# Two matmuls in place of three for the mixers' projections, the halves of the output added on ScalarE and VectorE

## The chip, the cores and the metric

The kernel runs on one core of a Trainium2 chip. The metric is the time of one execution on the device in microseconds, the median of several runs. TensorE (PE) multiplies out of SBUF into PSUM; ScalarE (ACT), VectorE (DVE) and GpSimd (POOL) work on tiles of 128 partitions; SyncE (SP) starts the DMA transfers. Each engine takes its instructions in the order of its own queue.

## The reference, cut to what matters

Two layers; each is a SwiGLU FFN, a mixing block and a second FFN, on 256 tokens of 1024 features in float32.

```
u = rms_norm(h, ln_mix[l])
z, xbc, dt_raw, cq, ckv, kr, gates = split_cols(u @ w_in[l], IN_SPLIT_SIZES)
y_ssd = ssd_branch(z, xbc, dt_raw, ...)      # conv + silu of xbc, chunked scan, gated by silu(z), norm, @ w_ssd_out
y_mla = mla_branch(cq, ckv, kr, cos, sin, ...)   # norm(cq) @ w_uq, norm(ckv) @ w_ukv, 8 heads, @ w_mla_out
g = jax.nn.sigmoid(gates.astype(jnp.float32)).astype(h.dtype)
merged = g[..., :D_MODEL] * y_ssd + g[..., D_MODEL:] * y_mla
h = h + merged @ w_o[l]
```

## The kernel before

All products with weights are made in float32r, in which an operand is split in a high part and a low part. An activation tile `X` holds for each 128 features both parts side by side, 256 columns each (`operand` writes them: ScalarE casts the high part, VectorE subtracts it for the low part). A weight block, 128 output features of 1024 input features as a rule, is loaded by one DMA into `st`; `ahead` casts it on ScalarE to `wh` (L151) and subtracts on VectorE to `wl` (L152). There are four buffers each of `st`, `wh` and `wl`, so a block is split when TensorE has finished the fourth block before it. The product is high x high + high x low + low x high, accumulated over the eight tiles of 128 input features in one of four PSUM buffers `g` (`gps`), which are used in turn.

Two helpers issue it. `mm` (L168 to L170) uses three matmuls of 256 columns for each tile of weights: `wh` with the high part, `wh` with the low part, `wl` with the high part, all into the same 256 columns. `mm2` (L177, L178) streams both parts of X behind one load of `wh`, 512 columns, and then `wl` with the high part, 256 columns into the first half; the two halves of the buffer add up to the product, and `halves` (L181, L182) adds them: a ScalarE copy of the second half to SBUF and a VectorE add of the first half. The FFNs, the gates inside the mixing block and `wso` use `mm2`; the dt and rotary key block `dk`, the first two gates, the six latents `lat`, the convolved blocks `bc` and `xs`, the blocks `z`, and `wmo` and `wo` use `mm`. So does the last output tile of all, which doesn't change.

The mixing block `mix` begins with the row factor of the tokens (`row_factor`: a sum over features on TensorE, L240, then nine small VectorE instructions, L248 and L215 to L223), while TensorE runs dk, two gates and latent 0. VectorE then splits weights, writes the scaled operand X for the loop (L454, L458), and the latents' operands into tile A (L204). `query` (L694) and `keyval` (L718) multiply these latents with the up-projections; each takes two PSUM buffers. Then comes the loop over eight steps of the scan (`ssd`, in which L632 writes xdt) and eight heads, with blocks of bc, xs, z and gates among them, then the merge (wso and wmo for eight output tiles) and wo. The instructions of each engine are put in order ahead of time by a scheduler with its own model of durations; on the chip each engine goes through its queue in that order.

Of the kernel before, what the change touches and what calls it, by code (L numbers as in the profile page):

```python
# [39 lines left out]
# columns of the per-layer vector block  # L40
# [15 lines left out]
# columns of the constant block  # L56
# [4 lines left out]
class Build:  # L61
# [17 lines left out]
    def plan(self):  # L79
        """every weight block in the order of its use"""  # L80
# [62 lines left out]
    def ahead(self, most=WBUF):  # L143
        """loads blocks and splits each in two float32r parts, ahead of their use"""
        while self.split_n < min(self.used + most, len(self.blocks)):
            k, src, n, w = self.blocks[self.split_n]
            st = self.stp.tile([P, 1024], F32, name="st", tag="st")[:, :n]
            self.nc.sync.dma_start(st, src)
            wh = self.whp.tile([P, 1024], F32R, name="wh", tag="wh")[:, :n]
            wl = self.wlp.tile([P, 1024], F32R, name="wl", tag="wl")[:, :n]  # L150
            self.nc.scalar.copy(wh, st)  # L151
            self.nc.vector.tensor_tensor(out=wl, in0=st, in1=wh.bitcast(F32), op=ALU.subtract)  # L152
            self.ready[self.split_n] = (k, wh.rearrange("p (k c) -> p k c", c=w), wl.rearrange("p (k c) -> p k c", c=w))
            self.split_n += 1
# [17 lines left out]
    def mm2(self, out, w, nk, X, x0, start, stop):  # L172
        """one load of the high weights serves both parts of X; the halves of out add up to the product"""
        wh, wl = w
        mm = self.nc.tensor.matmul
        for k in range(nk):
            mm(out, lhsT=wh[:, k, :], rhs=X[:, x0 + k, :], start=start and k == 0, stop=False)  # L177
            mm(out[:, :T], lhsT=wl[:, k, :], rhs=X[:, x0 + k, :T], start=False, stop=stop and k == nk - 1)  # L178
# [28 lines left out]
    def rsqrt(self, x, n, tag):  # L207
        """1 / sqrt(x): exponent trick, one tuned Newton step, one step of third order"""
# [26 lines left out]
    def row_ms(self, acc, scale, tag):  # L235
        """mean of squares + eps, tokens on partitions: [P, 2]"""
# [133 lines left out]
    def post_h(self, n, X, gain):  # L370
        """square and operand of feature tile n of the residual for the next block"""
        if n == 0:
            self.acc = self.tmp("acc", [P, T], bufs=1)
        self.operand(X, n, self.hT[:, n, :], gain[:, n:n + 1])
        self.square_into(self.acc, self.hT[:, n, :], n == 0)

# [42 lines left out]
    def mix(self, l, X0, Xn, gain, gain_next):  # L419
# [9 lines left out]
        def latent(i):  # L429
            q = int(i > 3)  # L430
            ps = self.gps()[:, :T]
            self.mm(ps, self.w("lat"), KD, X0, 0, True, True)
            o = V_QL + i
            self.operand(A, 16 + i, ps, v[:, o:o + 1])
            self.square_into(acc2[q], ps, i in (0, 4))

# [1 line left out]
        with self.tc.issue_after(self.last):  # L438
            ps = self.gps()[:, :T]
            self.mm(ps, self.w("dk"), KD, X0, 0, True, True)  # L440
            pg = self.gps()
            for g in range(2):
                self.mm(pg[:, g * T:(g + 1) * T], self.w("gate"), KD, X0, 0, g == 0, g == 1)
            latent(0)
        Rb = self.bcast(Rt, None)
        gg = self.tmp("g0", [P, 2, T], bufs=1)
        nc.scalar.copy(gg, pg.rearrange("p (g t) -> p g t", g=2))
        dk = self.tmp("ta", [P, T])
        nc.scalar.copy(dk, ps)
# [106 lines left out]
        for n in range(KD):  # L556
# [9 lines left out]
            ps = self.gps()[:, :T]  # L566
            self.mm(ps, self.w("wmo"), 8, oT, 0, True, True)
            tt(out=m, in0=gg[:, 1, :], in1=ps, op=ALU.mult)
            tt(out=m, in0=m, in1=gg[:, 0, :], op=ALU.add)
            self.operand(M, n, m)  # L570
        for n in range(KD):
            ps = self.gps()[:, :T]
            self.mm(ps, self.w("wo"), 8, M, 0, True, True)
            tt(out=self.hT[:, n, :], in0=self.hT[:, n, :], in1=ps, op=ALU.add)
# [11 lines left out]
    def conv_pair(self, S, key, cis, out):  # L586
        """out = 2 * silu(conv) for two feature tiles"""
        nc, v = self.nc, S["v"]
        y = self.tmp("cy", [P, 2, T])
        for i, ci in enumerate(cis):  # L590
            ps = self.gps()[:, :T]
            self.mm(ps, self.w(key), KD, S["X"], 0, True, True)
# [72 lines left out]
    def z(self, S, j):  # L665
        nc = self.nc
        ps = self.gps()
        for i in range(2):
            self.mm(ps[:, i * T:(i + 1) * T], self.w("z"), KD, S["X"], 0, i == 0, i == 1)
        ps = ps.rearrange("p (g t) -> p g t", g=2)  # L670
        z = self.tmp("zz", [P, 2, T], bufs=ZB)
        nc.scalar.activation(out=z, in_=ps, func=AF.Tanh, scale=0.5)
        nc.vector.scalar_tensor_tensor(out=z, in0=z, scalar=1.0, in1=ps, op0=ALU.add, op1=ALU.mult)
# [10 lines left out]
    def query(self, S, p):  # L684
        """queries of two heads, tokens on partitions"""
# [21 lines left out]
    def keyval(self, S, p):  # L707
        """keys and values of two heads, tokens on partitions; the row factors of queries and keys"""
# [132 lines left out]
def _pack(w, nb):  # L841
    """[L, K, N] -> [L, N/(128 nb), 128, nb * K/128 * 128]: one contiguous run per partition and chunk"""
# [66 lines left out]
```

## Time and profile before

| what | value |
|---|---|
| time, median of 3 runs | 1484.74 us (1484.6 to 1485.36) |
| profiled execution: span from first to last instruction | 1480.6 us |
| median less that span | 4.1 us |
| TensorE, VectorE, ScalarE busy | 1469.6, 1119.8, 908.6 us |
| granted TensorE clock, mean | 1.000 |

The page gives no other time for the profiled execution than its span; the median is that of executions timed without the profile. A matmul's end is modelled in the trace, and a matmul overlaps the next, so the price of one is read from the starts of a run of them, not from its duration.

### The profile page before, as it was taken

Reading aid. Unit: us, or ns where it says so; the run is one execution under the profiler, and the core shown is the slowest. Engines: PE = TensorE matmul, PEld = TensorE weight load, DVE = VectorE, ACT = ScalarE, POOL = GpSimd, SP = SyncE. Lnnn points to the kernel's source line nnn. Section 1 sums busy time; section 2 is a strip of 40 time slices with the busy share of each in tenths; the row PEclk is TensorE's granted clock in tenths of the full one; section 3 lists DMA queues with packets and bytes.
Section 4 is the critical chain, followed back from the end, with each engine's and each line's share of the span. In section 5 each row is a group of like instructions: output and inputs, shape, how many; then the busy total and the mean of one; then the engine's idle time right before and its main releaser. Section 6 shows DMA issues by size and latency. Waiting matters only on the chain.

```text
span 1480.6 us, 25069 instructions
## 1 busy us (share of the span) xinstructions
PE 1469.6 (99%) x9482; PEld 1313.5 (89%) x9482; DVE 1119.8 (76%) x2089; ACT 908.6 (61%) x1736; POOL 0.2 (0%) x4
## 2 busy tenths in 40 slices
PE   7999999999999999999999999999999999999999
PEld 6888899888888998888888888998888889988888
DVE  7877679888776667777677876898887676777764
ACT  6655566887765455555455554668787654555542
POOL 0000000000000000000000000000000000000000
PEclk9999999999999999999999999999999999999999
DMA  7555655333344555556655566553434445555563
GB/s 258 189 188 172 202 178 175 134 128 122 129 142 157 185 178 187 192 191 180 194 189 193 190 184 191 175 164 123 138 126 136 142 162 188 182 185 188 190 193 116
DMA packets 73353, 252.98 MB, mean 171 GB/s; under 512 B 8337, under 2 KB 10641, under 8 KB 73233
## 3 DMA queue, kind: packets, MB, share of 16 engines
q1 hardware_dynamic: 73232, 251.39, 52.7%
q8 instruction: 74, 1.21, 0.3%
q14 instruction: 47, 0.38, 0.1%
HBM read 250.31 MB, written 1.05 MB: 170 GB/s over the span
## 4 chain that ended last, share of the span: by engine, by line
PE 99%; DMA 0%; DVE 0%; ACT 0%; issue 0%; SPq 0%; ACTq 0%; DVEq 0%
PE g L177 40%; PE g L178 20%; PE g L168 9%; PE g L169 9%; PE g L170 9%; PE g L694 2%; PE s L657 2%; PE g L718 2%; PE h L779 1%; PE h L778 1%; PE s L640 1%; PE h L802 1%; PE h L760 0%; PE s L629 0%; PE h L798 0%; DMA hT<-in_x_dram 0%
## 5 line engine op out<-in xcount | busy, mean ns | idle before, releaser
L151 ACT CAST wh<-st 128x1024 fp32r<-128x1024 f32 (+2 forms) x488 | 502.9, 1031 | 495.2 <-PE g L177 309.1
L152 DVE TENSOR_TENSOR wl<-st,wh 128x1024 fp32r<-128x1024 f32 (+2 forms) x488 | 581.5, 1192 | 258.8 <-ACT wh L151 254.5
L177 PE MATMUL g<-X,wh 128*128 128x512 f32 x928 | 329.3, 397 | 7.9 <-DVE X L204 7.5
L177 PE MATMUL g<-A,wh 128*128 128x512 f32 x938 | 327.6, 395 | 0.0
L178 PE MATMUL g<-X,wl 128*128 128x256 f32 x928 | 263.1, 284 | 0.0
L178 PE MATMUL g<-A,wl 128*128 128x256 f32 x938 | 260.6, 278 | 0.0
L177 PE MATMUL g<-oT,wh 128*128 128x512 f32 x704 | 244.5, 392 | 0.0
L168 PE MATMUL g<-X,wh 128*128 128x256 f32 x768 | 220.5, 288 | 0.0
L169 PE MATMUL g<-X,wh 128*128 128x256 f32 x768 | 219.7, 286 | 0.0
L170 PE MATMUL g<-X,wl 128*128 128x256 f32 x768 | 218.5, 285 | 0.0
L177 PEld LDWEIGHTS g<-X,wh 128*128 128x128 f32 x928 | 175.3, 189 | 47.8 <-DVE X L204 8.2
L177 PEld LDWEIGHTS g<-A,wh 128*128 128x128 f32 x938 | 175.7, 188 | 40.1
L178 PE MATMUL g<-oT,wl 128*128 128x256 f32 x704 | 196.9, 280 | 0.0
L178 PEld LDWEIGHTS g<-X,wl 128*128 128x128 f32 x928 | 176.9, 191 | 1.2 <-issue 0.3
L178 PEld LDWEIGHTS g<-A,wl 128*128 128x128 f32 x938 | 176.6, 188 | 0.4
L177 PEld LDWEIGHTS g<-oT,wh 128*128 128x128 f32 x704 | 131.6, 187 | 28.6
L168 PEld LDWEIGHTS g<-X,wh 128*128 128x128 f32 x768 | 146.3, 191 | 2.9 <-issue 1.5
L169 PEld LDWEIGHTS g<-X,wh 128*128 128x128 f32 x768 | 146.5, 191 | 2.4 <-issue 0.7
L170 PEld LDWEIGHTS g<-X,wl 128*128 128x128 f32 x768 | 146.5, 191 | 0.7 <-issue 0.2
L178 PEld LDWEIGHTS g<-oT,wl 128*128 128x128 f32 x704 | 133.0, 189 | 0.2
L170 PE MATMUL g<-oT,wl 128*128 128x256 f32 x272 | 76.8, 285 | 0.0
L169 PE MATMUL g<-oT,wh 128*128 128x256 f32 x272 | 76.7, 283 | 0.0
(288 smaller groups left out, 1849.1 us busy)
## 6 DMA issues: line engine op xcount, KB each, us to landing
st<-in_w_dram SPq DMA_DIRECT2D x238, 512.0 KB, 4.3
st<-in_win_dram SPq DMA_DIRECT2D x124, 512.0 KB, 3.8
st<-in_wso_dram SPq DMA_DIRECT2D x32, 512.0 KB, 4.2
st<-in_w_dram SPq DMA_DIRECT2D x32, 384.0 KB, 3.2
st<-in_wmo_dram SPq DMA_DIRECT2D x16, 512.0 KB, 4.1
st<-in_wo_dram SPq DMA_DIRECT2D x16, 512.0 KB, 3.5
st<-in_wuq_dram SPq DMA_DIRECT2D x16, 384.0 KB, 3.3
st<-in_wukv_dram SPq DMA_DIRECT2D x8, 512.0 KB, 3.8
```

Source lines behind the costliest of these rows:

```text
L151: self.nc.scalar.copy(wh, st)
L152: self.nc.vector.tensor_tensor(out=wl, in0=st, in1=wh.bitcast(F32), op=ALU.subtract)
L168: mm(out, lhsT=wh[:, k, :], rhs=xh, start=start and k == 0, stop=False)
L169: mm(out, lhsT=wh[:, k, :], rhs=xl, start=False, stop=False)
L170: mm(out, lhsT=wl[:, k, :], rhs=xh, start=False, stop=stop and k == nk - 1)
L177: mm(out, lhsT=wh[:, k, :], rhs=X[:, x0 + k, :], start=start and k == 0, stop=False)
L178: mm(out[:, :T], lhsT=wl[:, k, :], rhs=X[:, x0 + k, :T], start=False, stop=stop and k == nk - 1)
L640: nc.tensor.matmul(pbs[q][:, i * T:(i + 1) * T], lhsT=self.E[64 * q:64 * q + 64, h:h + 1].to_broadcast([64, P]), rhs=S["HL"][64 * q:64 * q ...
L657: nc.tensor.matmul(py[64 * i:64 * i + 64, q * T + c * P:(q + 1) * T], lhsT=xdt[:, c, f:f + 64], rhs=r[:, i, o:o + n], start=q == 0 and c = ...
L694: nc.tensor.matmul(pc[c], lhsT=aa, rhs=ww, start=k == 0 and i == 0, stop=k == 3 and i == 2)
L718: nc.tensor.matmul(pc[c], lhsT=aa, rhs=ww[:, k, :], start=k == 0 and i == 0, stop=k == 1 and i == 2)
L778: mm(o, lhsT=qkT[:, 0, cs], rhs=qkT[:, 1, ks], start=c == 0, stop=False)
```

## The change

The nine projections that used `mm` in the mixing block use `mm2`, each with a full PSUM buffer of 512 columns. `halves` puts the sum into an SBUF tile, and what read PSUM before reads this tile: the latents' operand and square (tile `cy`, two buffers), the convolution (tile `sq`, two buffers), z (its own tile), dk, the first gates, and the product with `wmo`. For `wo` there is no tile: VectorE adds both halves to the residual `hT` in two instructions. The two copies that emptied the first gates and dk are gone. z takes two PSUM buffers where two groups shared one. Lines of comment fell out of the file too, and line numbers shift by up to 7.

```diff
         def latent(i):
             q = int(i > 3)
-            ps = self.gps()[:, :T]
-            self.mm(ps, self.w("lat"), KD, X0, 0, True, True)
+            ps = self.gps()
+            self.mm2(ps, self.w("lat"), KD, X0, 0, True, True)
+            lat = self.tmp("cy", [P, 2, T])[:, 0, :]
+            self.halves(lat, ps)
             o = V_QL + i
-            self.operand(A, 16 + i, ps, v[:, o:o + 1])
-            self.square_into(acc2[q], ps, i in (0, 4))
+            self.operand(A, 16 + i, lat, v[:, o:o + 1])
+            self.square_into(acc2[q], lat, i in (0, 4))
...
         with self.tc.issue_after(self.last):
-            ps = self.gps()[:, :T]
-            self.mm(ps, self.w("dk"), KD, X0, 0, True, True)
-            pg = self.gps()
+            ps = self.gps()
+            self.mm2(ps, self.w("dk"), KD, X0, 0, True, True)
+            dk = self.tmp("ta", [P, T])
+            self.halves(dk, ps)
+            gg = self.tmp("g0", [P, 2, T], bufs=1)
             for g in range(2):
-                self.mm(pg[:, g * T:(g + 1) * T], self.w("gate"), KD, X0, 0, g == 0, g == 1)
+                ps = self.gps()
+                self.mm2(ps, self.w("gate"), KD, X0, 0, True, True)
+                self.halves(gg[:, g, :], ps)
             latent(0)
         Rb = self.bcast(Rt, None)
-        gg = self.tmp("g0", [P, 2, T], bufs=1)
-        nc.scalar.copy(gg, pg.rearrange("p (g t) -> p g t", g=2))
-        dk = self.tmp("ta", [P, T])
-        nc.scalar.copy(dk, ps)
...
-            ps = self.gps()[:, :T]
-            self.mm(ps, self.w("wmo"), 8, oT, 0, True, True)
-            tt(out=m, in0=gg[:, 1, :], in1=ps, op=ALU.mult)
+            ps = self.gps()
+            self.mm2(ps, self.w("wmo"), 8, oT, 0, True, True)
+            self.halves(m, ps)
+            tt(out=m, in0=gg[:, 1, :], in1=m, op=ALU.mult)
...
-            ps = self.gps()[:, :T]
-            self.mm(ps, self.w("wo"), 8, M, 0, True, True)
-            tt(out=self.hT[:, n, :], in0=self.hT[:, n, :], in1=ps, op=ALU.add)
+            ps = self.gps()
+            self.mm2(ps, self.w("wo"), 8, M, 0, True, True)
+            for o in (0, T):
+                tt(out=self.hT[:, n, :], in0=self.hT[:, n, :], in1=ps[:, o:o + T], op=ALU.add)
...
         for i, ci in enumerate(cis):
-            ps = self.gps()[:, :T]
-            self.mm(ps, self.w(key), KD, S["X"], 0, True, True)
+            pg = self.gps()
+            self.mm2(pg, self.w(key), KD, S["X"], 0, True, True)
+            ps = self.tmp("sq", [P, T])
+            self.halves(ps, pg)
...
-        ps = self.gps()
+        z = self.tmp("zz", [P, 2, T], bufs=ZB)
         for i in range(2):
-            self.mm(ps[:, i * T:(i + 1) * T], self.w("z"), KD, S["X"], 0, i == 0, i == 1)
-        ps = ps.rearrange("p (g t) -> p g t", g=2)
-        z = self.tmp("zz", [P, 2, T], bufs=ZB)
-        nc.scalar.activation(out=z, in_=ps, func=AF.Tanh, scale=0.5)
-        nc.vector.scalar_tensor_tensor(out=z, in0=z, scalar=1.0, in1=ps, op0=ALU.add, op1=ALU.mult)
+            ps = self.gps()
+            self.mm2(ps, self.w("z"), KD, S["X"], 0, True, True)
+            self.halves(z[:, i, :], ps)
+        th = self.tmp("t2", [P, 2, T])
+        nc.scalar.activation(out=th, in_=z, func=AF.Tanh, scale=0.5)
+        nc.vector.scalar_tensor_tensor(out=z, in0=th, scalar=1.0, in1=z, op0=ALU.add, op1=ALU.mult)
```

The scheduler puts the new instructions into the queues. On VectorE, at the head of layer 0's mixing block, this stood around the operand of latent 3 (L204 that reads g_2292; g_2251 is latent 2, g_2341 latent 4; L152 splits weights, L458 writes X):

```order
L204 SCALAR_TENSOR_TENSOR A_2068<-g_2251,vec0_85,A_2068 128x256
L508 TENSOR_SCALAR dtd_2459<-dte_2456 128x64
L233 TENSOR_TENSOR Rb_2069<-Rb_2069,sq_2243 128x256
L152 TENSOR_TENSOR wl_2345<-st_2342,wh_2344 128x768
L204 SCALAR_TENSOR_TENSOR A_2068<-g_2292,vec0_85,A_2068 128x256
L458 TENSOR_TENSOR X_2204<-t2_2287,X_2204 128x2x256
L458 TENSOR_TENSOR X_2204<-t2_2328,X_2204 128x2x256
L509 RECIPROCAL dtd_2459<-dtd_2459 128x64
L152 TENSOR_TENSOR wl_2379<-st_2376,wh_2378 128x1024
L204 SCALAR_TENSOR_TENSOR A_2068<-g_2341,vec0_85,A_2068 128x256
L559 TENSOR_SCALAR g0_2200<-g0_2200 128x256
```

and this now, at the add and the operand of latent 3 (PSUM buffer g_2258, sum in cy_2281; cy_2245 holds latent 2):

```order
L510 TENSOR_SCALAR dtd_2410<-dte_2407 128x64
L460 TENSOR_TENSOR X_2180<-t2_2253,X_2180 128x2x256
L152 TENSOR_TENSOR wl_2335<-st_2332,wh_2334 128x1024
L460 TENSOR_TENSOR X_2180<-t2_2289,X_2180 128x2x256
L561 TENSOR_SCALAR g0_2097<-g0_2097 128x256
L152 TENSOR_TENSOR wl_2452<-st_2449,wh_2451 128x1024
L182 TENSOR_TENSOR cy_2281<-cy_2281,g_2258 128x256
L511 RECIPROCAL dtd_2410<-dtd_2410 128x64
L204 SCALAR_TENSOR_TENSOR A_2068<-cy_2245,vec0_85,A_2068 128x256
L233 TENSOR_TENSOR Rb_2069<-Rb_2069,sq_2250 128x256
L512 TENSOR_TENSOR dte_2407<-dte_2407,dtd_2410 128x64
L204 SCALAR_TENSOR_TENSOR A_2068<-cy_2281,vec0_85,A_2068 128x256
```

Both last X operands (L460) and two splits of 1024 columns now stand ahead of what first reads latent 3; the operands of latents 2 and 3 stand behind its add.

On TensorE, at the end of latent 5 (g_2331) and the start of the query block (L701, L694 before), the queue now reads as follows; g_2461 and g_2462 are the query's two PSUM buffers, in turn those of latents 2 and 3:

```order
L178 MATMUL g_2331<-oT_1558,wl_2226 128x256
L701 MATMUL g_2461<-wh_2261,A_2068 128x384
L701 MATMUL g_2461<-wl_2262,A_2068 128x384
L701 MATMUL g_2461<-wh_2261,A_2068 128x384 x2
L701 MATMUL g_2461<-wl_2262,A_2068 128x384
L701 MATMUL g_2461<-wh_2261,A_2068 128x384
L701 MATMUL g_2461<-wh_2305,A_2068 128x384
L701 MATMUL g_2461<-wl_2306,A_2068 128x384
L701 MATMUL g_2462<-wh_2261,A_2068 128x384
L701 MATMUL g_2462<-wl_2262,A_2068 128x384
```

Eight matmuls into the first buffer now stand ahead of the first into the second. Earlier in this queue, the row sum L240 stood behind 44 matmuls of the triples of dk and the first gate, and stands behind 35 matmuls of pairs now.

## Rows read from the trace of the kernel before

**Rows 1.** The page: the span, and each engine's busy time, share and instructions.

```profile
span 1480.6 us, 25069 instructions
PE 1469.6 (99%) x9482; PEld 1313.5 (89%) x9482; DVE 1119.8 (76%) x2089; ACT 908.6 (61%) x1736; POOL 0.2 (0%) x4
```

**Rows 2.** The page: the chain that ended last, share by engine and by line.

```profile
PE g L177 40%; PE g L178 20%; PE g L168 9%; PE g L169 9%; PE g L170 9%; PE g L694 2%; PE s L657 2%; PE g L718 2%; PE h L779 1%; PE h L778 1%; PE s L640 1%; PE h L802 1%; PE h L760 0%; PE s L629 0%; PE h L798 0%; DMA hT<-in_x_dram 0%
```

**Rows 3.** Waits of TensorE: us in total, times, longest.

```profile
PE g L177 <- DVE X L204: 7.5, 2, 7.0
```

**Rows 4.** Timeline of TensorE: start, duration, instruction; gates, then the merge.

```profile
420.65 0.40 PE L177 MATMUL g<-X,wh 128*128 128x512 f32 x1
...
421.71 0.40 PE L177 MATMUL g<-X,wh 128*128 128x512 f32 x1
...
500.79 0.28 PE L168 MATMUL g<-oT,wh 128*128 128x256 f32 x1
...
503.67 0.40 PE L177 MATMUL g<-A,wh 128*128 128x512 f32 x1
...
509.32 0.28 PE L168 MATMUL g<-oT,wh 128*128 128x256 f32 x1
```

**Rows 5.** Timeline of TensorE in the second FFN of layer 0.

```profile
570.46 0.40 PE L177 MATMUL g<-oT,wh 128*128 128x512 f32 x1
...
599.93 0.39 PE L177 MATMUL g<-oT,wh 128*128 128x512 f32 x1
```

**Rows 6.** Groups of instructions by line: count, busy us, mean ns.

```profile
L168 PE MATMUL g<-X,wh 128*128 128x256 f32 x768 | 220.5, 288 | 0.0
L168 PE MATMUL g<-oT,wh 128*128 128x256 f32 x272 | 76.4, 283 | 0.0
```

**Rows 7.** One line of `halves`: count, duration in ns (min/median/max), first and last start.

```profile
L181 ACT COPY t<-g x180: 355/358/383, 13.5 to 1417.4; 128x256 f32<-128x256 f32 x180
```

**Rows 8.** Two stretches: length, busy us (instructions) of PE, PEld, DVE, ACT, POOL.

```profile
203.00:223.00 20.00, 20.00 (x169) 20.00 (x169) 19.93 (x45) 14.91 (x31) 0.00 (x0) 1.00 0.60 194
203.00:273.00 70.00, 70.00 (x549) 67.80 (x549) 65.12 (x162) 51.36 (x114) 0.00 (x0) 1.00 0.53 175
```

**Rows 9.** Timeline of VectorE in layer 0; in brackets the idle time and its releaser.

```profile
201.71 0.16 DVE L248 TENSOR_SCALAR rhm<-s 128x2 f32<-128x2 f32 x1 [3.26 <-PE s L240]
...
203.36 3.49 DVE L152 TENSOR_TENSOR wl<-st,wh 128x1024 fp32r<-128x1024 f32 x3
...
218.99 0.42 DVE L233 TENSOR_TENSOR Rb<-Rb,sq 128x256 f32<-128x256 f32 x1
219.33 0.95 DVE L152 TENSOR_TENSOR wl<-st,wh 128x768 fp32r<-128x768 f32 x1
220.20 0.48 DVE L204 SCALAR_TENSOR_TENSOR A<-g,vec,A 128x256 fp32r<-128x256 f32 x1
220.59 1.28 DVE L458 TENSOR_TENSOR X<-t,X 128x512 fp32r<-128x512 f32 x2
221.79 0.55 DVE L509 RECIPROCAL dtd<-dtd 128x64 f32<-128x64 f32 x1
...
224.26 1.22 DVE L152 TENSOR_TENSOR wl<-st,wh 128x1024 fp32r<-128x1024 f32 x1
225.39 0.23 DVE L510 TENSOR_TENSOR dte<-dte,dtd 128x64 f32<-128x64 f32 x1
...
272.50 0.75 DVE L632 TENSOR_TENSOR xdt<-s,dth 128x256 f32<-128x256 f32 x2
```

**Rows 10.** Timeline of TensorE in layer 0: mixing block's start, row sum, query.

```profile
195.90 0.28 PE L168 MATMUL g<-oT,wh 128*128 128x256 f32 x1
...
201.17 0.50 PE L240 MATMUL s<-ones,acc 128*128 128x1 f32 x4
...
222.89 0.34 PE L694 MATMUL g<-wh,A 128*128 128x384 f32 x1
223.07 0.34 PE L694 MATMUL g<-wl,A 128*128 128x384 f32 x1
```

## The prediction

> **What bounds the kernel now.** The page comes first: in a span of 1480.6 us TensorE is busy for 99%, VectorE for 76% and ScalarE for 61% [rows 1]. The chain that ended last consists of TensorE's matmuls: 60% of it are the two of `mm2`, 27% the three of `mm` [rows 2]. The list of waits then says whether TensorE ever stands still for another engine: 7.5 us in two waits for an operand, 7.0 of them once [rows 3], and hardly more. So whatever shortens TensorE's stream shortens the kernel, and whatever makes it wait lengthens it by as much, because no idle time is left in which a loss could be made good.
>
> The timed median is 1484.74 us and the profiled span 1480.6; I work with differences, and put them on the median (4.1 us lie outside the span).
>
> **What the change gives on TensorE.** `mm` costs three matmuls of 256 columns for each 128 rows of weights, `mm2` one of 512 and one of 256: 768 columns either way, so only the fixed part of one matmul can go. The starts in the timeline give the price: eight triples from 500.79 to 503.67, 360 ns each; the sixteen pairs behind them up to 509.32, 353 ns each [rows 4]. In the next FFN 85 pairs run from 570.46 to 599.93, 347 ns each [rows 5]. Gate pairs among the small matmuls of the mixer are at the slower rate: three from 420.65 to 421.71, 353 ns each [rows 4]. I have no cause for the two rates. The slower one is seen behind triples, which the mixers will no longer have, and also among small matmuls, which stay; so I take 350, between them. The change turns 768 + 272 = 1040 triples into pairs [rows 6] (the 22 on A, the last output tile, stay). The gain is 1040 x 10 ns = 10.4 us, with ends 1040 x 6.9 = 7.2 and 1040 x 13.3 = 13.8.
>
> The Trainium skill, in TensorE: Matmul & The Clock Gate, "Back-to-back issue gap", speaks against the change: an isolated matmul takes its columns at 2.4 GHz plus about 2.5 ns, so a saved matmul would be worth 2.5 ns and the gain 2.6 us. The trace does not agree: 120 ns per matmul of a triple is 13 above 256 columns at 2.4 GHz, and the pairs are shorter by 7 to 13.
>
> **What it adds on the other engines.** Per layer 65 groups of eight triples are converted (130 x 8 = 1040). 57 get `halves`, one ScalarE copy and one VectorE add; the 8 of `wo` get a second VectorE add. The copy lasts 0.36 us in the FFN [rows 7]. The add is an instruction of the shape of L233, behind which the next starts after 0.34 us in a full queue [rows 9] (the L233 at 218.99). So VectorE gains 130 x 0.34 = 44 us of work and ScalarE at most 114 x 0.36 = 41, less four copies dropped. Tanh and product of z read SBUF where they read PSUM, 16 times; even 0.1 us each is 1.6 us on engines with hundreds to spare. Over the whole span both fit in their idle time (VectorE 361 us of it), so the average says that they cost nothing. The stages decide.
>
> **Where the cover is missing.** In the 20 us from 203 on VectorE is busy for 19.93, in the 70 us from there for 65.12 [rows 8]: at the head of the mixer it is full while the dt, key, gate and six latent groups come. Nine of the new adds fall there. I follow the queue of layer 0.
> 1. The row sum, L240, stood behind 44 matmuls of triples, at 201.17, 5.27 us after the mixer begins at 195.90 [rows 10]; now it stands behind 35 matmuls of pairs, 17.5 x 0.347 = 6.1 us. VectorE, which waited for it 3.26 us [rows 9], starts its rsqrt 0.8 us later.
> 2. From the first split behind the rsqrt, 203.36, to the operand of latent 3 at 220.20 VectorE took 16.84 us without a hole [rows 9]. The new queue has, up to the end of the add of latent 3: seven adds more (dk, two gates, four latents), 2.4 us; two weight splits ahead of it that stood behind, 2 x 1.13 by the one at 224.26; the last two X operands, 1.2 by those at 220.59; and one L204 fewer, 0.39 by that at 220.20 [rows 9]. That is 16.84 + 2.4 + 2.3 + 1.2 - 0.4 = 22.3 us, so the add ends at 203.36 + 0.8 + 22.3 = 226.5. (ScalarE, at 14.91 of the 20 us [rows 8], is not in its way.)
> 3. The query block takes two of the four PSUM buffers, those of latents 2 and 3. Before, the operand of latent 3 was there at 220.7, and the query began at 222.89 with a matmul every 0.18 us [rows 9, 10]. Now TensorE is there 72 x 10 ns = 0.7 us sooner, at 222.2, does the eight matmuls that stand ahead of the second buffer's first, and from 223.6 waits until 226.5: **2.9 us**. All else on TensorE is queued behind it.
> 4. Key and value need latent 5, whose add comes out of the same full queue behind two more operands, two more adds and a split, 2 x 0.39 + 2 x 0.34 + 1.13 and small ones, 3 to 4 us behind that of latent 3; its cast and low part follow. TensorE gets there some 4 us after 226.5. The two are level, and I add **1 us**.
>
> Layer 1 has the same order without the next layer's constants. So about 4 us a layer, **8 us** in both, with ends 0 (the second rival) and the 15 us of the first. Behind this place the splits stand ahead of the adds in the queue, and a conv's buffer comes free after one copy and one add, where an Identity and three products read it.
>
> Other places: `wmo` puts a copy and an add, at most 0.36 + 0.34 us, into the chain to M, and `wo` an add into that to the next FFN's operand. Both are hidden by the matmuls that the next group can do with the seven tiles it has, 7 x 0.35 = 2.4 us; if they are not, they cost 0.7 and 0.34 a layer, 2 us in all. I take 0. z holds two PSUM buffers in place of one, each for a shorter time. DMA traffic and the order of weights do not change.
>
> **Sum.** 1484.7 - 10.4 + 8 = 1482.3; I say **1482**.
>
> **Rivals.**
> - *VectorE stays the bound up to the second scan step* (slower). Before, its 69.1 us from 203.36 to the second xdt at 272.50 [rows 9] held 4.9 us of idle [rows 8]; 20 adds now fall ahead of that point, 6.8 us. If the idle can be squeezed out the work ends at 204.2 + 71 = 275, no worse than the 4 us above; if it stays, at 280.1, and a layer loses 7.6. Then 1484.7 - 10.4 + 15.2 = 1489.5. It decides from 5.2 us of loss a layer on. For it: nothing pulls a strict queue together; against it: TensorE has up to four blocks of split weights in hand there. 0.25.
> - *The wait is hidden*: TensorE gets the latents in time, and the gain stays whole, 1474, with 347 ns pairs 1471. Against it stands the count of step 2; for it, that TensorE never waited in a stretch in which VectorE was full. 0.20.
> - *Columns alone count on TensorE* (the change doesn't do what it says): a pair among small matmuls takes a triple's 360 ns, nothing is gained, and with 8 us of waits the time is 1492. The gate rows at 420 us speak against it [rows 4]; for it speaks only that they are few. 0.10. The Trainium skill's rule above, in TensorE: Matmul & The Clock Gate, "Back-to-back issue gap", comes close to this: its 2.6 us would make 1490; by it the trace does not go, as said.
>
> **Chances and range.** My forecast has 0.45. Its own range is 1476 to 1488 (pairs 347 to 353, waits 5 to 11 us). I take 3 us, 0.2%, as what a measurement tells from no change. The forecast gives 0.21 faster, 0.19 same and 0.05 slower; the hidden wait 0.20 faster; the full VectorE 0.20 slower and 0.05 same; the last 0.10 slower. Sums: 0.41, 0.24, 0.35. The range over the cases: 1473, just under the hidden wait, to 1491, past the full VectorE and short of the 15 us with 353 ns pairs.
>
> **What would show it.** Pairs in the mixers start every 347 to 353 ns, and no L168 is left but on A. TensorE's waits name VectorE's L182 at the query, some 3 us in each layer (at about 223 us in layer 0), and TensorE's busy share falls there alone. If its waits stay under 2 us in all, step 2 is wrong; if waits for L182, or for weights, go on past 235 us, the first rival holds. If all engines are in time and the span is no shorter, the pair's price was misread.

## The result, and the profile after

The changed kernel takes 1497.52 us (median of four, 1497.22 to 1498.29) beside 1485.05 us before: a ratio of 1.0088 with the 95% interval 1.0076 to 1.0100. It is 12.5 us slower. The forecast was 1482 us, with a range up to 1491.

The page of the profile after, with the lines that answer to [rows 1] and [rows 2]:

```profile
span 1495.7 us, 23229 instructions
...
PE 1471.7 (98%) x8442; PEld 1259.3 (84%) x8442; DVE 1162.7 (78%) x2219; ACT 940.0 (63%) x1846; POOL 0.2 (0%) x4
...
PE 95%; DVE 2%; ACT 2%; issue 0%; DMA 0%; SPq 0%; DVEq 0%; ACTq 0%
PE g L177 55%; PE g L178 28%; PE g L701 2%; PE s L663 2%; PE g L725 1%; PE h L786 1%; PE h L785 1%; PE s L646 1%; DVE wl L152 1%; PE h L809 0%; ACT wh L151 0%; PE s L635 0%; PE h L767 0%; PE h L805 0%; ACT dec L653 0%; PE s L614 0%
```

1040 of TensorE's 9482 matmuls are gone, and it is busy for 2 us longer. VectorE has 43 us more to do and ScalarE 31, where 44 and at most 41 less four copies were counted. VectorE and ScalarE now have 2% each of the chain that ended last. TensorE's longest waits (us in total, times, longest), where before there was only the first of them [rows 3] and one of 0.5 us, also in the first FFN:

```profile
PE g L177 <- DVE X L204: 7.6, 2, 7.1
PE g L701 <- DVE cy L182: 3.4, 2, 1.7
PE h L785 <- ACT qkT L769: 2.4, 2, 1.4
PE s L663 <- DVE dec L656: 2.2, 1, 2.2
PE g L701 <- ACT A L203: 1.2, 2, 0.8
PE h L809 <- ACT pT L807: 1.1, 2, 0.6
PE h L805 <- ACT pp L802: 0.9, 1, 0.9
PE g L177 <- DVE sq L182: 0.7, 1, 0.7
```

L701 is the query, L663 the scan, L785 to L809 the heads of attention; `sq` at L177 is a conv's sum. The query's waits were forecast. The 6.6 us of the scan and the heads, and the conv's 0.7, were not.

**The head of the mixing block, layer 0.** TensorE's timeline (start, duration, instruction, in brackets the idle time and its releaser), to be held against [rows 10]:

```profile
198.68 0.40 PE L177 MATMUL g<-oT,wh 128*128 128x512 f32 x1
...
204.81 0.50 PE L240 MATMUL s<-ones,acc 128*128 128x1 f32 x4
...
225.56 0.41 PE L701 MATMUL g<-wh,A 128*128 128x384 f32 x1
...
227.30 0.45 PE L701 MATMUL g<-wh,A 128*128 128x384 f32 x1 [0.46 <-ACT A L203]
227.58 0.34 PE L701 MATMUL g<-wl,A 128*128 128x384 f32 x1
229.66 0.41 PE L701 MATMUL g<-wh,A 128*128 128x384 f32 x1 [1.74 <-DVE cy L182]
...
232.56 0.52 PE L701 MATMUL g<-wl,A 128*128 128x384 f32 x1
232.88 0.52 PE L701 MATMUL g<-wh,A 128*128 128x384 f32 x1
233.20 0.52 PE L701 MATMUL g<-wl,A 128*128 128x384 f32 x1
```

VectorE's queue from the row sum to the add of latent 3, against [rows 9]:

```profile
205.34 0.16 DVE L248 TENSOR_SCALAR rhm<-s 128x2 f32<-128x2 f32 x1 [4.12 <-PE s L240]
...
206.99 1.22 DVE L152 TENSOR_TENSOR wl<-st,wh 128x1024 fp32r<-128x1024 f32 x1
...
229.10 0.41 DVE L182 TENSOR_TENSOR cy<-cy,g 128x256 f32<-128x256 f32 x1
```

The second PSUM buffer of the query is released by the add of latent 3, as the prediction said. Behind the wait the matmuls of 384 columns start every 0.32 us (232.56, 232.88, 233.20), where before it was 0.18 [rows 10]. The stretches of 2 us there (length; busy us of PE, PEld, DVE, ACT, POOL; granted clock; DMA share; GB/s) say why:

```profile
226.00:228.00 2.00, 1.46 (x7) 0.82 (x5) 2.00 (x5) 1.55 (x4) 0.00 (x0) 1.00 0.55 195
228.00:230.00 2.00, 0.34 (x2) 0.37 (x3) 2.00 (x5) 0.45 (x2) 0.00 (x0) 1.00 0.70 215
230.00:232.00 2.00, 2.00 (x10) 2.00 (x9) 1.95 (x7) 1.55 (x4) 0.00 (x0) 0.65 0.69 215
232.00:234.00 2.00, 2.00 (x8) 2.00 (x7) 1.73 (x4) 1.23 (x4) 0.00 (x0) 0.50 0.27 104
234.00:236.00 2.00, 2.00 (x12) 1.47 (x10) 1.16 (x4) 1.92 (x7) 0.00 (x0) 1.00 0.63 186
```

TensorE works for 1.80 us of the 4 from 226, and behind that its granted clock is at 0.50, which is the lower level of 1.2 GHz, until 234. What was lost to the clock is (1 - 0.65) x 2 + (1 - 0.50) x 2 = 1.7 us. In layer 1 the same happens at the query, and once more in the loop, behind a wait of 1.44 us at 1033. All such rows of this execution add up to 6.8 us. The Trainium skill, in TensorE: Matmul & The Clock Gate, "HAM oscillation — how this bites in real kernels", tells of waits that bring the clock down again and again, and counts half of the time at the lower level as lost. These rows agree, with starts 0.32 us apart in place of 0.18, but the waits here, 0.46 and 1.74 us, are shorter than those of the kernel it describes.

**The stages, before and after**, from the starts of their first matmuls, in us, layer 0 / layer 1:

| stage | before | after | change |
|---|---|---|---|
| first FFN | 188.9 / 184.0 | 191.6 / 184.0 | +2.7 / 0 |
| head of the mixing block, to the first matmul on X | 34.4 / 34.4 | 38.8 / 39.2 | +4.4 / +4.7 |
| the rest of the block up to the merge | 238.3 / 237.8 | 240.6 / 240.7 | +2.3 / +2.9 |
| merge and wo | 92.1 / 92.0 | 90.7 / 91.3 | -1.4 / -0.7 |

Head, loop (the rest of the block), merge and wo make +12.2 us, beside 12.5 between the medians. The 2.7 us of layer 0's first FFN, in code that the change does not touch, are left out of this, for a reason that stands in the last section.

### The profile page after: what moved, and what is told of

Same layout as the page of the kernel before. It is cut to its first block, busy times and chain, and to the rows that moved or that the text cites. A ratio compares the mean times of both kernels' runs of the same rounds, so it can differ in the third digit from the quotient of the medians.

```text
span 1495.7 us, 23229 instructions
## 1 busy us (share of the span) xinstructions
PE 1471.7 (98%) x8442; PEld 1259.3 (84%) x8442; DVE 1162.7 (78%) x2219; ACT 940.0 (63%) x1846; POOL 0.2 (0%) x4
## 4 chain that ended last, share of the span: by engine, by line
PE 95%; DVE 2%; ACT 2%; issue 0%; DMA 0%; SPq 0%; DVEq 0%; ACTq 0%
PE g L177 55%; PE g L178 28%; PE g L701 2%; PE s L663 2%; PE g L725 1%; PE h L786 1%; PE h L785 1%; PE s L646 1%; DVE wl L152 1%; PE h L809 0%; ACT wh L151 0%; PE s L635 0%; PE h L767 0%; PE h L805 0%; ACT dec L653 0%; PE s L614 0%
## 5 line engine op out<-in xcount | busy, mean ns | idle before, releaser
L152 DVE TENSOR_TENSOR wl<-st,wh 128x1024 fp32r<-128x1024 f32 (+2 forms) x488 | 581.5, 1192 | 243.6 <-ACT wh L151 239.8
L177 PE MATMUL g<-X,wh 128*128 128x512 f32 x1696 | 608.1, 401 | 9.3 <-DVE X L204 7.6
L177 PEld LDWEIGHTS g<-X,wh 128*128 128x128 f32 x1696 | 320.1, 189 | 84.9 <-DVE X L204 8.4
L177 PE MATMUL g<-oT,wh 128*128 128x512 f32 x976 | 341.2, 393 | 0.0
L177 PE MATMUL g<-A,wh 128*128 128x512 f32 x938 | 327.3, 394 | 0.0
L177 PEld LDWEIGHTS g<-oT,wh 128*128 128x128 f32 x976 | 182.6, 187 | 40.9
L177 PEld LDWEIGHTS g<-A,wh 128*128 128x128 f32 x938 | 175.6, 188 | 40.6
L178 PEld LDWEIGHTS g<-oT,wl 128*128 128x128 f32 x976 | 184.3, 189 | 0.5 <-DVE wl L152 0.3
L182 DVE TENSOR_TENSOR t<-t,g 128x256 f32<-128x256 f32 x180 | 74.0, 413 | 0.0
L603 DVE SCALAR_TENSOR_TENSOR cy<-sq,vec,cy 128x255 f32<-128x255 f32 (+1 forms) x144 | 67.5, 476 | 3.2 <-ACT cy L600 2.7
L181 ACT COPY t<-g 128x256 f32<-128x256 f32 x180 | 65.0, 364 | 0.2 <-PE g L178 0.2
L398 DVE TENSOR_TENSOR t<-t,Rb 128x512 f32<-128x512 f32 x88 | 60.1, 684 | 0.2
L653 ACT ACTIVATE dec<-s,acum 128x256 f32<-128x256 f32 (+1 forms) x128 | 43.8, 442 | 4.0 <-PE s L646 3.9
L701 PE MATMUL g<-wh,A 128*128 128x384 f32 x128 | 38.6, 368 | 4.7 <-DVE cy L182 3.4
```

Of the source, the lines that this page charges most:

```text
L181: self.nc.scalar.copy(out, ps[:, T:])
L182: self.nc.vector.tensor_tensor(out=out, in0=out, in1=ps[:, :T], op=ALU.add)
L398: nc.vector.tensor_tensor(out=gu, in0=gu, in1=Rb2, op=ALU.mult)
L603: nc.vector.scalar_tensor_tensor(out=y[:, i, k:], in0=ps[:, :T - k], scalar=v[:, w0 + 3 - k:w0 + 4 - k], in1=y[:, i, k:], op0=ALU.mult, op ...
L653: act(out=r[:, i, o:o + n], in_=pb[:, i * T + c * P:(i + 1) * T], func=AF.Relu, scale=-1.0, bias=S["acum"][:, c, h:h + 1])
L701: nc.tensor.matmul(pc[c], lhsT=aa, rhs=ww, start=k == 0 and i == 0, stop=k == 3 and i == 2)
```

## The experiments

The table gives each kernel's time, that of the kernel before in the same session, the ratio with its interval, and from the profile, all behind layer 0's first FFN: TensorE's idle time (gaps over 0.1 us between the end of a matmul and the start of the next; before has none there), and what the half clock took ((1 - granted clock) x length, summed over stretches of 2 us up to the last matmul). The rest is what the stretch became longer or shorter by beyond these two: where matmuls were saved and nothing else happened it is the gain, as a negative number. It also holds the change of the small matmuls between the large ones, and in run 6 the 22 added ones. In runs 4 and 10 TensorE stood idle for 5.8 and 3.4 us of the time at half clock, so there 2.9 and 1.7 us are counted in both columns; without that their rest is -2.3 and -8.6.

| kernel | us | before | ratio (95%) | waits | clock | rest |
|---|---|---|---|---|---|---|
| the change | 1497.5 | 1485.1 | 1.0088 (1.0076 to 1.0100) | 12.5 | 6.8 | -7.0 |
| 1, pairs, nothing added | 1480.4 | 1484.7 | 0.9971 (0.9962 to 0.9981) | 3.3 | 1.7 | -8.7 |
| 2, wmo and wo alone | 1480.9 | 1484.7 | 0.9976 (0.9967 to 0.9984) | 0 | 0 | -3.9 |
| 3, head alone | 1493.7 | 1484.7 | 1.0061 (1.0045 to 1.0076) | 4.8 | 3.4 | 1.3 |
| 4, loop alone | 1495.9 | 1484.7 | 1.0079 (1.0065 to 1.0092) | 8.3 | 8.5 | -5.2 |
| 5, triples with the added work | 1496.3 | 1485.3 | 1.0072 (1.0058 to 1.0086) | 8.4 | 1.7 | 1.2 |
| 6, matmuls fill the wait | 1502.0 | 1485.3 | 1.0115 (1.0101 to 1.0129) | 10.7 | 11.9 | -4.2 |
| 7, bc 0 ahead of the query | 1489.3 | 1485.3 | 1.0025 (1.0015 to 1.0035) | 6.9 | 0 | -2.2 |
| 8, z, wmo and wo | 1485.9 | 1485.3 | 0.9998 (0.9989 to 1.0007) | 3.1 | 1.7 | -3.5 |
| 9, ScalarE's copy alone | 1481.1 | 1484.5 | 0.9970 (0.9958 to 0.9983) | 3.4 | 1.7 | -9.2 |
| 10, one VectorE copy alone | 1492.3 | 1484.5 | 1.0056 (1.0041 to 1.0072) | 11.7 | 6.8 | -10.3 |
| 11, splits on GpSimd | 1514.4 | 1484.5 | 1.0202 (1.0188 to 1.0216) | 25.4 | 6.8 | -3.7 |
| 12, bc first, loop on triples | 1486.6 | 1484.5 | 1.0016 (1.0007 to 1.0025) | 4.5 | 0 | -1.6 |

**1. The pairs without what they add.**

```diff
             self.mm2(ps, self.w("lat"), KD, X0, 0, True, True)
-            lat = self.tmp("cy", [P, 2, T])[:, 0, :]
-            self.halves(lat, ps)
+            lat = ps[:, :T]
```

(and so in all nine projections; dk and the first gates are copied out of PSUM by ScalarE again, as before, and z has its tanh and its product in two halves)

> All nine projections of the mixing block on pairs, but nothing is done with the second half of a buffer (high x low is left out of these products): no copy, no add, readers take the first half from PSUM as before. Theory A (pairs gain 7 to 13 ns for each of the 1040 triples wherever no engine is waited for; the loss comes from the added copies and adds): 1485 - 7 to 13 = 1472 to 1478, head of the mixer 0.7 us shorter than its 34.45, loop 2.2 to 4.2 us shorter than its 238, clock 1.00. Theory B (columns alone count, pairs give nothing in the mixers): 1485, no stage shorter by more than 0.5 us.

1480.4 us: 4.3 us faster, neither theory's number. Behind the first FFN the profiled stretch is 3.7 us shorter; 3.3 us of new waits and 1.7 of half clock are in it, so 8.7 us were gained on TensorE, 8.4 ns a triple. The pairs are worth what was forecast (7 to 13 ns); but even without an added instruction the new order of the queues brings waits, the longest of 1.9 us in layer 1's loop.

**2. wmo and wo alone.** The edit is the part of the change in the merge and wo, without the rest.

> Only wmo and wo on pairs (32 of the 130 groups), the rest as before. Theory A: -32 x 8 x 7 to 13 ns = -1.8 to -3.3 us, so 1481.7 to 1483.2, all of it between the end of the loop and the FFN. Theory B: 1485. If the first FFN of layer 0, which no edit touches, is again at 191.6 instead of 188.9 us, its rate is a matter of the program as a whole and not of the changed place.

3.8 us faster, by the profile 2.0 and 2.1 in the two layers, all of it there, and no new wait: TensorE's list has only the two entries of the first FFN. Theory A, and a little more than it gave, since the pairs of wso come to the faster rate as well, now that no triples stand between them. TensorE's timeline in the merge of this kernel shows the first matmuls of pairs of wso, which start every 0.34 to 0.35 us, where [rows 4] had 0.353:

```profile
489.66 0.39 PE L177 MATMUL g<-A,wh 128*128 128x512 f32 x1
...
490.00 0.39 PE L177 MATMUL g<-A,wh 128*128 128x512 f32 x1
...
490.35 0.39 PE L177 MATMUL g<-A,wh 128*128 128x512 f32 x1
```

**3 and 4. The head alone, the loop alone.** Each is the part of the change in its place, the rest as before.

> Only dk, the first two gates and the six latents on pairs (18 groups), the rest as before. Theory A (the adds in VectorE's full queue make the query late, and the clock falls to half behind the wait): heads 38 to 39 us instead of 34.45, so +8 to +9, 1493 to 1494, with a granted clock near 0.5 for some 4 us behind the query in at least one layer; the loop back at about 238. Rival (the wait at the query is made good behind it, and the clock falls only with the loop's edits): at most +2, 1485 to 1487.

> Only bc, xs and z in the loop on pairs (80 groups), head and merge as before. Theory A (the loop's own copies and adds lie in the chains that TensorE's small matmuls wait for): heads at 34.45, loops 240 to 241 us instead of 238, waits of TensorE for dec, qkT, pp or pT of 3 us and more, so 1485 + 4 to 6 = 1489 to 1491. Rival (the loop only inherited a late head): loops 234 to 236, 1479 to 1481.

The head alone costs 9.0 us: its stages are 38.7 and 39.6 us long, with waits of 1.8 and 1.6 us for the adds, and 1.7 us lost to the clock in each layer. The loops stay at 238.8 and 237.0. The loop alone costs 11.2 us, with no change at the head (34.4 us), so it inherits nothing: its waits are its own. They are these, with the half clock of layer 0, which sets in while TensorE still waits and lasts behind it:

```profile
PE h L801 <- ACT pp L798: 5.9, 2, 3.0
PE s L659 <- DVE dec L652: 2.1, 2, 1.0
```

```profile
288.00:290.00 2.00, 0.00 (x0) 0.00 (x0) 1.86 (x4) 2.00 (x6) 0.00 (x0) 0.72 0.45 164
290.00:292.00 2.00, 1.08 (x3) 0.47 (x3) 1.30 (x7) 2.00 (x7) 0.00 (x0) 0.50 0.33 72
292.00:294.00 2.00, 1.33 (x8) 0.77 (x8) 2.00 (x7) 2.00 (x5) 0.00 (x0) 0.50 0.31 124
294.00:296.00 2.00, 2.00 (x9) 1.63 (x7) 2.00 (x6) 0.32 (x1) 0.00 (x0) 0.58 0.00 0
```

The three parts alone make 9.0 + 11.2 - 3.8 = 16.4 us, the whole 12.5: head and loop together cost less than one by one.

**5. The added work without the pairs.**

```diff
+    def same(self, out, ps):
+        self.nc.scalar.copy(out, ps[:, :T])
+        self.nc.vector.tensor_tensor(out=out, in0=out, in1=ps[:, :T], op=ALU.max)
...
-            self.mm2(ps, self.w("lat"), KD, X0, 0, True, True)
+            self.mm(ps[:, :T], self.w("lat"), KD, X0, 0, True, True)
...
-            self.halves(lat, ps)
+            self.same(lat, ps)
```

> Triples everywhere in the mixing block as before, but the added work of the change is put behind each group all the same: a ScalarE copy and a VectorE maximum with the same columns (for wo a second VectorE instruction), which leaves the values as they are. Theory A (the copies and adds in the queues of ScalarE and VectorE make TensorE wait, and the clock falls behind the waits; the pairs themselves give some 7 to 10 us back): slower than the changed kernel, 1500 to 1508, waits of TensorE of 6 us and more, clock 0.997 or less. Rival (the pairs bring the waits, because TensorE arrives earlier than ScalarE and VectorE can serve it): at most 3 us over before, 1485 to 1488.

11.0 us slower, below theory A's range and far above the rival's; its executions lie between 1492.9 and 1498.1. The work, with the buffers of the change, makes 8.4 us of waits with TensorE as slow as before. Heads are 36.6 and 35.5 us long, loops 242.1 and 241.5. Against before, the changed kernel loses 1.4 us more than this one, which the intervals do not resolve: of the time that TensorE saves by its pairs nothing arrives, since it waits 4.1 us more and loses 5.1 us more to the clock.

**6. The wait filled.**

```diff
         pc = [self.gps()[:, :2 * QK] for _ in range(2)]
+        if p == 0:
+            fill = self.hps()
+            for _ in range(11):
+                nc.tensor.matmul(fill, lhsT=blocks[0][0][:, 0, :P], rhs=self.X0[:, 0, :], start=True, stop=True)
```

> The changed kernel with eleven matmuls of 512 columns that nobody reads ahead of the first query of each layer, about as long (2.3 us) as TensorE waits there. Theory A (the wait costs twice: its own length, and the half clock behind it): no wait at the query, granted clock 1.00 from there on, heads 36 to 37 us instead of 38.8 and 39.2, the whole 4 us less, about 1493, if the loop stays as it is. Rival (the clock has nothing to do with it, and what follows the query waits anyway): heads stay at 38.5 us or more.

Theory A fell in its number, and so did the rival. The waits at the query are gone and the clock holds through it, but right behind it TensorE waits 1.5 us (layer 0) for ScalarE's copy of the query and in that layer the clock falls there; the heads are 37.5 and 38.0 us long, not 36 to 37. In the loop, which the edit does not touch, the queues came out in another order: layer 0's is 247.9 us long where the change has 240.6, and 11.9 us are lost to the clock in all. So the order that the scheduler gives can move a loop by 7 us with the same work in it, and every edit here draws a new order. What a wait at the query costs by the clock alone is therefore read from the rows, and was not measured by itself.

**7. bc 0 ahead of the query.**

```diff
-        order = [("query", 0), ("keyval", 0), ("bc", 0), ("xs", 0)]
+        order = [("bc", 0), ("query", 0), ("keyval", 0), ("xs", 0)]
```

> The changed kernel with the blocks of bc 0 ahead of the first query and keys instead of behind them (weights and instructions). Theory A (the query comes before VectorE has added the latents, and 5.6 us of matmuls that need none of them cover that): no wait for the latents' L182, granted clock 1.00 up to the scan, 7 to 9 us less than the changed kernel, 1488 to 1491. Rival (VectorE's queue is the bound there, and the wait only moves to X or to the conv's buffers): 1495 to 1498.

1489.3 us, 8.2 less than the changed kernel, as theory A gave. No wait at the query is left and the clock is at 1.00 in every stretch behind the first FFN. The two blocks of bc 0, which need none of the latents, give VectorE the time that its queue lacks there. What remains are waits in the loop for the scan's factors, and 0.5 us in each layer for the add of a latent, now within bc 0, ahead of the query:

```profile
PE s L663 <- DVE dec L656: 3.8, 4, 1.1
PE g L177 <- DVE cy L182: 1.0, 2, 0.5
```

**8. z with wmo and wo.** The edit leaves out the head and the conv of the change.

> z, wmo and wo on pairs, head and conv as before. Theory A (the conv's copy and add stand in the chain to the scan and make the loop's waits, z has time): the tail's 3.8 us and 256 triples x 10 ns of z, 1478 to 1479, no new wait of TensorE. Rival (z's two PSUM buffers and its copies are what disturbs the loop): 1484 or more, waits for pp, dec or qkT as in the loop alone.

No difference from before, the rival's number, though not its waits: z takes back the 3.8 us of wmo and wo and its own gain. One wait of 1.9 us for `sm L796` (VectorE) in layer 0, with 1.7 us of clock behind it, and pairs of wso and wmo at the slower rate of 0.353 us make it. So the conv is not alone in it: z does harm as well.

**9 and 10. One engine at a time.** In all places of the change but `wo`:

```diff
+    def half(self, out, ps):
+        self.nc.scalar.copy(out, ps[:, :T])
...
-            self.halves(lat, ps)
+            self.half(lat, ps)
```

That is run 9, in which `wo` adds the first half alone. In run 10 the line in `half` is `self.nc.vector.tensor_copy(out, ps[:, :T])`.

> Everything on pairs as in the change, but of the added work only ScalarE's copy is left, of the first half of each buffer; VectorE adds nothing (high x low is left out of these products). Theory A (VectorE's queue is what TensorE waits for, as the prediction had it): heads under 36 us, waits of TensorE under 4 us, 1481 to 1486, near the kernel in which both are left out. Rival (ScalarE's queue and the hop over it make the waits): 1491 or more.

> Everything on pairs as in the change, but a single VectorE copy of the first half takes the place of ScalarE's copy and VectorE's add (high x low is left out; wo keeps its two adds). Theory A (VectorE's queue): heads 38 us and more, waits at the query for this copy, 1492 to 1498. Rival (ScalarE): heads under 36 us, 1481 to 1487. If both this and the copy alone are fast, it is the hop over two engines that makes the waits, not the load of either.

For the kernel as a whole the two answer the question which engine it is. With ScalarE's copy the kernel takes 1481.1 us, 0.6 more than with neither (run 1), though the copies come at the same places with 31 us of ScalarE's time. With the VectorE copy, and nothing on ScalarE, it takes 1492.3, 7.8 us over before. The change is 12.5 over before: what makes the other 5, with ScalarE's copy ahead of VectorE's add, no run separates. By stage the two are less clear. Heads are 35.3 and 35.9 us long with ScalarE's copy, 38.2 and 36.5 with VectorE's; the loops 234.1 and 237.5, and 242.3 and 237.4, so in layer 1's loop there is no difference. TensorE's longest waits with ScalarE's copy:

```profile
PE g L177 <- DVE X L207: 7.5, 2, 6.9
PE g L177 <- ACT vv L742: 1.8, 1, 1.8
PE h L770 <- ACT qn L713: 0.8, 1, 0.8
```

and with VectorE's:

```profile
PE h L808 <- ACT pp L805: 4.7, 1, 4.7
PE g L704 <- DVE A L207: 2.5, 3, 1.1
PE s L666 <- DVE dec L659: 1.6, 1, 1.6
```

The longest wait names ScalarE's `pp`, though ScalarE has in run 10 no more to do than before. VectorE's and ScalarE's timelines ahead of it, in layer 0's loop:

```profile
292.37 0.16 DVE L803 RECIPROCAL sm<-sm 128x2 f32<-128x2 f32 x1
...
293.79 2.58 ACT L656 ACTIVATE dec<-s,acum 128x256 f32<-128x256 f32 x8
...
297.02 0.83 ACT L805 ACTIVATE pp<-pp,sm 128x128 f32<-128x128 f32 x2
```

What `pp` needs of VectorE, `sm`, was there at 292.53; ScalarE, without a hole from 292.31 on, had a weight cast, eight `dec` and more ahead of `pp` in its queue, and came to it 4.5 us later. Before, 1.7 us lay between the two (283.48 and 285.16). Run 4's wait of 2.97 us is of the same kind: `sm` was ready at 286.72, `pp` began at 290.05. So neither wait is VectorE coming late with what was waited for; it is the order of ScalarE's queue in a kernel whose new work is on VectorE (run 10) or on both (run 4). How the one leads to the other was not shown.

**11. Weight splits on GpSimd.**

```diff
-            self.nc.vector.tensor_tensor(out=wl, in0=st, in1=wh.bitcast(F32), op=ALU.subtract)
+            eng = self.nc.gpsimd if k in ('lat', 'uq', 'ukv', 'bc', 'xs', 'z') and self.split_n % 2 else self.nc.vector
+            eng.tensor_tensor(out=wl, in0=st, in1=wh.bitcast(F32), op=ALU.subtract)
```

> The changed kernel, with the low part of every second weight block of the latents, uq, ukv, bc, xs and z subtracted on the idle GpSimd instead of VectorE, which loses some 28 x 1.15 = 32 us of work per layer, more than the 22 us that the change adds. Theory A (VectorE's load makes the waits): heads 35 to 36 us, loops 235 to 238, 1480 to 1488. Rival (GpSimd takes too long for a block, or slows VectorE): waits of TensorE for L152, 1500 or more.

The rival's number, by its second reason. GpSimd took 2.5 us for a split of 1024 columns, fast enough, and TensorE waits 1.6 us for splits, 1.3 of them in the first FFN; but VectorE, with 58 instructions fewer, is busy for 1190.6 us where the changed kernel has 1162.7. Instructions of its own became longer, for one the low part of the latents' operand. The groups by line (count, busy us, mean ns, idle time before) of this kernel:

```profile
L153 POOL TENSOR_TENSOR wl<-st,wh 128x1024 fp32r<-128x1024 f32 x50 | 125.1, 2502 | 1021.9 <-ACT wh L151 999.1 <-PE s L481 8.6 <-PE s L647 8.1
...
L205 DVE SCALAR_TENSOR_TENSOR A<-cy,vec,A 128x256 fp32r<-128x256 f32 x12 | 10.8, 896 | 0.0
```

and of the changed kernel:

```profile
L204 DVE SCALAR_TENSOR_TENSOR A<-cy,vec,A 128x256 fp32r<-128x256 f32 x12 | 5.5, 469 | 0.0
```

So this run did not relieve VectorE, and says nothing against the theory of its queue; it agrees with it.

**12. A version meant to be the fastest.** Runs 7 and 2 with the head on pairs and the loop on triples.

> A version meant to be the fastest: head, wmo and wo on pairs, the loop's bc, xs and z on triples, and bc 0 ahead of the first query, which covers the latents. Theory A: the tail's 3.8 us and up to 1.4 us of the head, no wait at the query and no half clock, 1479.5 to 1481.5. Rival (bc 0 ahead of the query costs in the scan what it saves at the query, as the waits for dec in the run with bc first say): 1483 to 1489, waits for dec.

1486.6 us, slower than before: the rival's range, though not its wait. TensorE waits 1.3 us in each layer for `rob L357`, the query's rotary part, on VectorE, and 0.5 us for the add of a latent. With bc 0 ahead the head's adds are still not free; what moving bc 0 costs without them was not tried. Run 2 stays the fastest kernel that computes the reference, 0.24% below the one before.

## Why the prediction was wrong, step by step

- **What bounds the kernel.** TensorE, and whatever makes it wait lengthens the kernel: held. "By as much" did not: a wait can cost more than its length, since the clock fell behind it, 1.7 us a time or more.
- **The gain on TensorE**, 10.4 us with ends 7.2 and 13.8: the mechanism held, and so did the size where the added work was left out (8.7 and 9.2 us in runs 1 and 9). In the changed kernel it is 7.0, and run 3, the head alone, has no gain in its rest. The Trainium skill, in TensorE: Matmul & The Clock Gate, "Back-to-back issue gap", has a fixed 2.5 ns for an isolated matmul beside its columns. The prediction's estimate from it, 2.5 ns for each matmul saved, was not borne out: run 1 gave 8.4.
- **Steps 1 to 3.** L240 stands 204.81 - 198.68 = 6.13 us behind the block's start, forecast 6.1. The queue from the first split to the end of the add of latent 3 lasts 229.51 - 206.99 = 22.5 us, forecast 22.3. The wait is 0.46 + 1.74 = 2.2 us (2.4 in layer 1), forecast 2.9; TensorE came to the query 26.9 us after the block's start and not 26.3, because the pairs of the head gained 0.1 us up to there (0.4 in layer 1) and not 0.7. The count of instructions in a full queue was right to 1%.
- **Step 4**, 1 us at key and value: no such wait is in the list. In its place came the half clock, 1.7 us, which the prediction does not have. A head was to become 4 - 0.7 = 3.3 us longer and became 4.4 and 4.7: 2.5 us of the error.
- **"Behind this place the splits stand ahead of the adds in the queue, and a conv's buffer comes free after one copy and one add".** This is the step that failed: with it the waits of the loop got no term in the sum. The loop was to keep its gain of 320 x 10 ns = 3.2 us a layer and became 2.3 and 2.9 us longer: 11.6 us of the error of 15.5. The reasoning looked at who frees a buffer and not at what else stands behind the new instructions in the queues. In the 20 us from 283, 45.5 us behind the loop's first matmul, VectorE and ScalarE are nearly full and TensorE works for 16.53 us. In the same place before (first row) they had room:

```profile
275.80:295.80 20.00, 20.00 (x139) 16.91 (x139) 16.21 (x38) 14.86 (x37) 0.00 (x0) 1.00 0.37 119
...
283.00:303.00 20.00, 16.53 (x100) 12.23 (x98) 18.86 (x49) 17.99 (x52) 0.00 (x0) 1.00 0.33 101
```

  The scan's factor for which TensorE waits there, from 296.87 to 299.11, comes last out of VectorE (L656), which reads the first of two exponentials of ScalarE (L655):

```profile
296.57 1.62 ACT L655 ACTIVATE dec<-dec 128x768 f32<-128x768 f32 x2
...
298.10 0.95 DVE L656 TENSOR_TENSOR dec<-dec,cbm 128x768 f32<-128x768 f32 x1
```

  That exponential ended at 297.47. With VectorE free at once its 0.95 us would have ended at 298.42, so some 0.6 of the 2.24 us are VectorE's queue and 1.6 came with ScalarE, which has no hole from 291 on. Run 4 shows the loop's loss without the head's, run 5 without the pairs. Run 10 shows that VectorE's work alone makes 7.8 of the kernel's 12.5 us, run 9 that ScalarE's alone makes none. Which queue makes the loop's loss, and how much of it is the order drawn by the scheduler, is not shown.
- **wmo and wo hidden, "I take 0":** held. Run 2 has the gain whole and no wait.
- **The rivals.** *VectorE stays the bound up to the second scan step* named the right sign and, for the kernel as a whole, the right engine; it put the loss ahead of 272 us and at 7.6 a layer with the head's. It came at the head and then at 287 to 404, 1033 and 1140 to 1157, and in another form: not one stretch of full VectorE, but single waits, some of which stand behind ScalarE's queue. Its sign, waits for L182 or for weights past 235 us, was seen once each: 0.70 us for a conv's sum at 292 and 0.53 for weights at 288. *The wait is hidden* fell with the query's rows, *columns alone count* with run 1.
- **Base.** The 4.1 us between median and span held about 2 us that belong to the profiled execution: in each of the 20 executions of before in one session the time less the span was 2.1 to 2.2 us, and the spans went from 1479.8 to 1486.3. Since the sum was made of differences on the median, this moved nothing.

What stays open: which engine's queue makes the loop's loss, and which order of queues the loop would need for its pairs to pay; and the price of the clock by itself, since run 6 changed the loop with it.

## What to carry to other kernels

Work added to an engine with a quarter of its time free is not free where a full TensorE takes its operands from that engine's queue: ask at each place who stands behind the new instruction and how much slack that one has, stage by stage, and price a wait of TensorE with the clock that may fall behind it. Look at the queues of the other engines too: the last releaser's name says neither which engine is short nor why it came late. Convert the places one by one: here 32 of 130 groups gave 3.8 us, and the other 98 took 16. The run with the added work alone and the run with the saving alone, each one edit, tell more than the whole.

## What the runs showed of the hardware that was not expected

- **The clock fell behind short waits, and not behind all.** Behind 0.46 and 1.74 us of waiting within 3 us at the query it was at 0.50; behind the single wait of 2.24 us at 296.87 in the same execution it stayed at 1.00. The stretches at half clock in these profiles lost 1.7 us each, or two or three times that.
- **The same pairs run at two rates.** In layer 0's first FFN, whose code and data are the same in both kernels, the 100 us from 40 on held 579 of TensorE's instructions before and 568 after. Before:

```profile
40.00:140.00 100.00, 100.00 (x579) 88.15 (x578) 81.60 (x148) 58.93 (x109) 0.00 (x0) 1.00 0.58 188
```

  and after:

```profile
40.00:140.00 100.00, 100.00 (x568) 86.72 (x567) 79.93 (x144) 57.97 (x109) 0.00 (x0) 1.00 0.58 186
```

  at the same full clock without a wait: pairs every 346.7 and every 353.3 ns. This is the table's 2.7 us. It is not the change: run 2 and run 3, which leave other parts on triples, have the slower rate there too, run 4 the faster one. The profiled span of before, 1480.6, is near the lower end of the 1479.8 to 1486.3 that its executions showed, so most of them probably had the slower one. What sets the rate was not found.
- **GpSimd's subtraction of two SBUF tiles made VectorE's instructions beside it longer**, 469 to 896 ns in the mean of run 11's row. The adds that read PSUM (L183 there, into `sq`) stayed at 414 ns beside it, where they took 410 without.
